# Eight additions of BP, eight products with AG and two products with GP taken from GpSimd to VectorE in the routing of a one-core decoder layer

## The chip, the cores and the metric

One core of a Trainium2 chip runs the whole kernel. The metric is the device time of one execution in microseconds, from which a median over runs is taken: 1073.58 us over three runs (1069.57 to 1077.26). In what follows PE is the engine of the matrix products (TensorE), PEld its loading of weights, DVE the vector engine, ACT the scalar engine, POOL GpSimd, and SP the engine whose queue issues most of the DMAs.

## The reference

One decoder layer over 1024 tokens of width 1024. A mixer with three branches gives `mix`; then

```python
x  = layernorm(alpha * x + (1 + gate1) * mix, ln1_g, ln1_b)
h2 = x * (1 + scale2) + shift2
logits = h2 @ w_router + b_router          # 32 experts
weights, experts = softmax(top4(logits))
ffn = sum over the 4 experts of weight * expert(h2)   # clamped SwiGLU, inner width 256
x  = layernorm(alpha * x + (1 + gate2) * ffn, ln2_g, ln2_b)
```

## The kernel before

Work goes in tiles of 128 tokens (t = 0 to 7) on the 128 partitions, everything in 32-bit floats; products that need the precision are made of three products of split halves (`mm3`, L224 to L226). The schedule is written by hand: each engine runs its instructions in the order in which the program issues them, and waits in that order.

Up to about 425 us the mixer runs. Then comes the routing, a loop over i = 2 to 7 (its body is printed below). In round i PE multiplies tile i of the mixer's output with `w_out` in two halves (`mix_mm`, 24 products each), while the tile u of the round before (u = i - 1; tiles 0, 1 and 2 are taken in rounds 2 and 3) is normalised and routed:

- `ln_half` and `stats` (L1005 to L1016, DVE) add the residual and take mean and variance; `norm` (L1029, ACT) writes the normalised row over x.
- `h2_mul` (L1033) makes h2 = x times GP, where GP is (1 + scale2) times the gain of the first norm. `h2_out` (L1038) adds BP, the shift that belongs to it, and SP stores the rows to HBM (L1039), from where the experts gather them. `y_scale` (L1042) multiplies x in place with AG, alpha times that gain: the residual that the output starts from.
- `logits` (L1049, PE) multiplies the transposed row with the router's weights into PSUM bank 7. `route` (L1055 to L1072) takes the best four experts and the mask M. `places_mm` (L1096, L1097, PE) counts with M how many earlier tokens chose each expert. `row_of` (L1140 to L1150) turns this into `idx`, rows of a table in HBM; its scratch lies in bank 7 too, so the logits of the next tile can't start until `idx` of the tile before is made. `to_table` has POOL write the four pairs per token with indirect DMAs (L1156).
- `y_mm` and `y_add` (L1173, L1179) add the experts' biases to the scaled row; SP stores it (L1182).

From round 5 on the weights of the first expert are split beside it (`units`, L1225 on ACT, L1228 on DVE). After the loop stands code without a loop, called the tail below (L1574 to L1660 or so): it routes tile 7 and runs the first three blocks of the experts (block = up to 128 rows of one expert) between the steps. It has its own product with GP (L1601, DVE) and addition of BP (L1623, POOL), splits two quarters of the second expert's weights on POOL (`hls[2][1](G)`, `hls[3][1](G)`, L1228), gathers rows (L1284, POOL), scales tile 7 (L1042, POOL) and orders the experts by size on DVE (L1500 to L1527). AG lies in memory that the down weights of the second expert take over (`dn`, L220 on ACT, L221 on DVE). Then the blocks of all experts follow until about 1000 us, and the second norm.

Before the change POOL makes all additions of BP and all products with AG, and the products with GP of tiles 1 and 2; DVE makes the other products with GP.

Of the kernel before, what the change touches and what calls it, by code (L numbers as in the profile page):

```python
# [146 lines left out]
def body(ctx, tc, A, out, offs, dbg=None):  # L147
    nc = tc.nc
    V, G, SC, PE, SY = nc.vector, nc.gpsimd, nc.scalar, nc.tensor, nc.sync
# [51 lines left out]
    def slot(kind, shape, dt=F32):  # L201
        n = turn[kind] = turn.get(kind, -1) + 1
        tag = SLOTS[kind][n % len(SLOTS[kind])]
        full = [shape[0], 2048 if tag[0] == "r" else 1024] if kind in ("x", "o", "xT", "gu") else None
        pool = keep if kind == "tt" else bigp if tag == "big" else mb[0] if kind in ("sg", "up", "gs") or tag[:2] == "dn" else ph
        if full and len(shape) > 2:
            full = [shape[0], shape[1], full[1] // shape[1]]
        return pool.tile(shape, dt, tag=tag, name=kind, bufs=COUNT.get(tag, 1), padded_shape=full)
# [76 lines left out]
    for i in range(5, 24):  # L285
        g, t = i // 8, i % 8
# [310 lines left out]
    for i in range(5, 24):  # L597
        g, t = i // 8, i % 8
# [349 lines left out]
    BP = pw.tile([P, D], F32, name="BP")  # L948
    r3 = rtile(3)
    GP, g2 = r3[:, :D], [r3[:, D:D + 512], r3[:, D + 512:]]  # L950
    AG = pw.tile([P, D], F32, name="AG")
# [42 lines left out]
    tk = {}  # L994
# [35 lines left out]

    def h2_mul(t):
        h2 = pw.tile([P, D], F32, tag="h2", name="h2", bufs=2)
        (G if t in (1, 2) else V).tensor_mul(h2, tk[t]["x"], GP)  # L1033
        tk[t]["h2"] = h2

    def h2_out(t):
        h2 = tk[t]["h2"]
        G.tensor_add(h2, h2, BP)  # L1038
        SY.dma_start(h2_d[blk(t + 1), :], h2)  # L1039

    def y_scale(t):
        G.tensor_mul(tk[t]["x"], tk[t]["x"], AG)  # L1042

    def logits(t, ks):
        if 0 in ks:
# [107 lines left out]
    def to_table(idx, pair):  # L1153
        for k in range(TOPK):
            G.memset(gap, 0.0)
            s_ = G.indirect_dma_start(out=tab_d, out_offset=bass.IndirectOffsetOnAxis(ap=idx[:, k:k + 1], axis=0),  # L1156
                                      in_=pair[:, k, :], in_offset=None)
            for o_ in scat:
                tc.declare_no_dep(s_.ins, o_.ins, reason="other rows of the table")
            scat.append(s_)  # L1160
# [131 lines left out]
    for i in range(2, NT):  # L1292
# [8 lines left out]
        if i == 3:  # L1301
            h2_mul(1)
            h2_out(1)
            y_scale(1)
            route_w(1)
            places_mm(1)
# [17 lines left out]
        if i == NT - 1:  # L1324
            gather(0)
        h2_mul(u)
        h2_out(u)
        y_scale(u)
        logits(u, range(KC))
        mix_mm(b, i, 1, range(2, 6))  # L1330
# [242 lines left out]
    t, w = NT - 1, NT - 2  # L1573
# [25 lines left out]
    x = tk[t]["x"]  # L1599
    h2 = pw.tile([P, D], F32, tag="h2", name="h2", bufs=2)  # L1600
# [19 lines left out]
    hls[0][1](V)  # L1620
    mring.allow(12)
    to_table(tk[t]["idx"], tk[t]["pair"])
    G.tensor_add(h2, h2, BP)  # L1623
    SY.dma_start(h2_d[blk(t + 1), :], h2)
    route_w(t)
    gu_mm(1)
# [10 lines left out]
    act_T(1, up)  # L1637
    gather(3)
    y_scale(t)
    gu_mm(2, range(0, 4))  # L1640
    for v in (w, t):
# [90 lines left out]
    with tc.For_i(0, n_over) as i:  # L1732
# [11 lines left out]
        x = slot("x", [P, D])  # L1744
# [124 lines left out]
```

## Time and profile before

| | |
|---|---|
| median of 3 runs | 1073.58 us |
| the profiled execution: its own time | 1075.12 us |
| the profiled execution: span from the first to the last instruction | 1073.3 us |
| PE busy in the span | 963.5 us (90%) |
| DVE busy | 812.4 us (76%) |
| ACT busy | 491.5 us (46%) |
| POOL busy | 370.8 us (35%) |
| mean granted clock of TensorE, as a share of full speed | 0.953 |

The profile is of one execution. A row of the chain or the timeline begins with the start of the instruction, counted from the start of the span, and its duration. What stands in brackets is the idle time of the engine just before it and what ended that. Shares of busy time are means over stages with different limits, so the routing is read by itself.

### The profile page before, as it was taken

The page shows a single profiled execution, that of the slowest core. Times are in us where ns is not written, and L with a number is a line of the kernel's source. Part 1 is how long each engine was busy: PE and PEld are TensorE (multiplying, and loading weights), DVE is VectorE, ACT ScalarE, POOL GpSimd, SP SyncE. Part 2 cuts the span into 40 slices and gives each one's busy share as a digit, 9 for nine tenths or more (in the row PEclk, how much of TensorE's full clock was granted, in tenths as well). Part 3 has the DMA queues.
Part 4 walks back from the last instruction along what each step waited for, and adds up shares of the span by engine and source line. Part 5 has one row for each costly group of instructions (what it writes and reads, how often), then busy time and mean ns, then how long its engine had stood idle before and what let it go on. Part 6 is the DMA issues. An engine that isn't in the chain of part 4 may idle for free. (4 is left out here: it accounts for less than half of the span.)

```text
span 1073.3 us, 14241 instructions
## 1 busy us (share of the span) xinstructions
PE 963.5 (90%) x4538; PEld 744.7 (69%) x4538; DVE 812.4 (76%) x1492; ACT 491.5 (46%) x788; POOL 370.8 (35%) x256
## 2 busy tenths in 40 slices
PE   5899999999999998699977999999998899997840
PEld 4777879778888777677866777777766577665520
DVE  5827669736577698757768689999979899888837
ACT  2263141322255444324452355665664556654636
POOL 2450011022000143677575322322433447544224
PEclk9899999999999999889989999999998999998975
DMA  9912127353443135314476989999989899998736
GB/s 311 325 47 79 60 79 258 111 196 125 140 144 103 45 106 183 103 40 143 158 255 217 272 256 299 338 297 320 286 274 298 247 327 302 306 279 263 236 71 270
DMA packets 115651, 219.20 MB, mean 204 GB/s; under 512 B 21166, under 2 KB 42680, under 8 KB 115576
## 3 DMA queue, kind: packets, MB, share of 16 engines
q1 hardware_dynamic: 99416, 181.50, 49.9%
q0 software_dynamic: 16160, 36.78, 14.9%
q8 instruction: 36, 0.59, 0.2%
q14 instruction: 39, 0.32, 0.1%
HBM read 187.27 MB, written 36.78 MB: 209 GB/s over the span
## 5 line engine op out<-in xcount | busy, mean ns | idle before, releaser
L1490 POOL DMA_INDIRECT y_d<-o,tt x46 | 88.4, 1922 | 197.6 <-DMA y_d<-o,tt 50.6
L1228 DVE TENSOR_TENSOR gu<-raw,gu 128x1024 fp32r<-128x1024 f32 x125 | 151.4, 1241 | 4.2 <-ACT gu L1225 3.9
L1225 ACT CAST gu<-raw 128x1024 fp32r<-128x1024 f32 x128 | 129.4, 1047 | 6.1 <-DMA raw<-in_w_gu 6.1
L1284 POOL DMA_INDIRECT x<-h_d,tt x46 | 91.8, 1996 | 92.2 <-PE bank L1396 67.1
L224 PE MATMUL bank<-gu,xT 128*128 128x512 f32 (+10 forms) x280 | 119.7, 428 | 0.0
L225 PE MATMUL bank<-gu,xT 128*128 128x512 f32 (+10 forms) x280 | 110.4, 394 | 2.1 <-DVE gu L1228 2.1
L226 PE MATMUL bank<-gu,xT 128*128 128x512 f32 (+10 forms) x280 | 110.9, 396 | 0.0
L226 PE MATMUL bank<-dn,aT 128*128 128x512 f32 (+11 forms) x184 | 75.6, 411 | 20.7 <-DVE aT L221 20.7
L224 PE MATMUL bank<-u,w 128*128 128x512 f32 x216 | 86.8, 402 | 0.0
L225 PE MATMUL bank<-u,w 128*128 128x512 f32 x216 | 85.3, 395 | 0.3 <-DVE u L221 0.3
L1484 DVE SCALAR_TENSOR_TENSOR o<-bank,tt,u 128x512 f32<-128x512 f32 (+11 forms) x92 | 65.5, 741 | 26.0 <-DMA y_d<-o,tt 17.9
L226 PE MATMUL bank<-u,w 128*128 128x512 f32 x216 | 85.0, 393 | 0.0
L220 ACT CAST dn<-raw 128x1024 fp32r<-128x1024 f32 x64 | 64.9, 1045 | 42.3 <-PE bank L226 35.1
L220 ACT CAST xT<-bank 128x512 fp32r<-128x512 f32 (+11 forms) x92 | 46.5, 508 | 76.5 <-PE bank L1396 74.5
L224 PE MATMUL bank<-w,u 128*128 128x512 f32 (+1 forms) x192 | 77.1, 402 | 2.8 <-ACT u L381 2.8
L221 DVE TENSOR_TENSOR dn<-raw,dn 128x1024 fp32r<-128x1024 f32 x64 | 76.0, 1213 | 2.9 <-ACT dn L220 2.6
L224 PE MATMUL bank<-dn,aT 128*128 128x512 f32 (+11 forms) x184 | 74.9, 407 | 0.4 <-ACT aT L220 0.4
L225 PE MATMUL bank<-dn,aT 128*128 128x512 f32 (+11 forms) x184 | 74.4, 404 | 0.0
L337 DVE SCALAR_TENSOR_TENSOR acc<-raw,cact,acc 128x512 f32<-128x512 f32 x80 | 68.2, 852 | 7.5 <-DMA raw<-in_w_ada 5.6
L226 PE MATMUL bank<-w,u 128*128 128x512 f32 (+1 forms) x192 | 71.5, 373 | 1.7 <-POOL u L382 1.6
L225 PE MATMUL bank<-w,u 128*128 128x512 f32 (+1 forms) x192 | 71.4, 372 | 1.1 <-DVE w L221 1.1
L224 PEld LDWEIGHTS bank<-gu,xT 128*128 128x128 f32 (+10 forms) x280 | 50.5, 180 | 18.9 <-issue 7.8
(419 smaller groups left out, 2197.5 us busy)
## 6 DMA issues: line engine op xcount, KB each, us to landing
raw<-in_w_gu SPq DMA_DIRECT2D x128, 512.0 KB
raw<-in_w_down SPq DMA_DIRECT2D x64, 512.0 KB
raw<-in_w_ada SPq DMA_DIRECT2D x32, 512.0 KB
raw<-in_w_ada SPq DMA_DIRECT2D x32, 256.0 KB
raw<-in_w_in SPq DMA_DIRECT2D x12, 512.0 KB
raw<-in_w_out SPq DMA_DIRECT2D x8, 512.0 KB
raw<-in_x SPq DMA_DIRECT2D x8, 512.0 KB
h_d<-h SPq DMA_DIRECT2D x8, 512.0 KB
```

Source lines behind the costliest of these rows:

```text
L220: SC.copy(hi, src)
L221: eng.tensor_tensor(lo, src, hi.bitcast(F32), op=ALU.subtract)
L224: PE.matmul(o, lh, rh, start=first, stop=False)
L225: PE.matmul(o, lh, rl, start=False, stop=False)
L226: PE.matmul(o, ll, rh, start=False, stop=last)
L337: V.scalar_tensor_tensor(acc, w[:, k, :], cact[:, kk:kk + 1], acc, op0=ALU.mult, op1=ALU.add)
L1225: SC.copy(hi_, r)
L1228: eng.tensor_tensor(lo_, r, hi_.bitcast(F32), op=ALU.subtract)
L1284: G.indirect_dma_start(out=x[:n], out_offset=None, in_=src, in_offset=bass.IndirectOffsetOnAxis(ap=segs[blocks[b]][:n, 0:1], axis=0), boun ...
L1484: V.scalar_tensor_tensor(o[:n, half_of(hf)], p_[:n], segs[s, i].bitcast(F32)[:n, 1:2], G2[:n, half_of(hf)], op0=ALU.mult, op1=ALU.mult)
L1490: G.indirect_dma_start(out=y_d, out_offset=bass.IndirectOffsetOnAxis(ap=segs[blocks[b]][:n, 0:1], axis=0), in_=outs.pop(b)[:n], in_offset= ...
```

## The change

Four lines: the calls of GpSimd (`G`) become calls of VectorE (`V`). The computation is the same; where the instructions stand in the program's order is the same too.

```diff
     def h2_mul(t):
         h2 = pw.tile([P, D], F32, tag="h2", name="h2", bufs=2)
-        (G if t in (1, 2) else V).tensor_mul(h2, tk[t]["x"], GP)
+        V.tensor_mul(h2, tk[t]["x"], GP)
         tk[t]["h2"] = h2

     def h2_out(t):
         h2 = tk[t]["h2"]
-        G.tensor_add(h2, h2, BP)
+        V.tensor_add(h2, h2, BP)
         SY.dma_start(h2_d[blk(t + 1), :], h2)

     def y_scale(t):
-        G.tensor_mul(tk[t]["x"], tk[t]["x"], AG)
+        V.tensor_mul(tk[t]["x"], tk[t]["x"], AG)
...
-    G.tensor_add(h2, h2, BP)
+    V.tensor_add(h2, h2, BP)
     SY.dma_start(h2_d[blk(t + 1), :], h2)
     route_w(t)
     gu_mm(1)
```

On DVE, at the start of round 3, the three instructions of tile 1 come to stand between `ln_half` of tile 3 and `route_w` of tile 1 (`raw` is x, `r` holds GP, `h` is h2, `es` the sum of the softmax):

```order
 L1005 SCALAR_TENSOR_TENSOR raw<-raw,bank 128x512
 L1006 BN_STATS stt<-raw 128x6
+L1033 TENSOR_TENSOR h_3934<-raw,r_3507 128x1024
+L1038 TENSOR_TENSOR h_3934<-h_3934,BP 128x1024
+L1042 TENSOR_TENSOR raw<-raw,AG 128x1024
 L1077 RECIPROCAL es<-es 128x1
 L1086 TENSOR_TENSOR bank<-bank,pairs 128x128
```

Three instructions are new ahead of everything that leads to `idx` of tile 1; the three of tile 2 follow right behind that `idx`, ahead of the tile's own route.

On DVE, in round 5 (tile 4; rounds 2, 4, 6 and 7 read alike), two instructions are new between the product with GP and the splitting of the expert's weights (`gu`) and the route:

```order
 L1006 BN_STATS stt<-raw 128x6
 L1033 TENSOR_TENSOR h_4372<-raw,r_3507 128x1024
+L1038 TENSOR_TENSOR h_4372<-h_4372,BP 128x1024
+L1042 TENSOR_TENSOR raw<-raw,AG 128x1024
 L1228 TENSOR_TENSOR gu<-raw,gu 128x1024
 L1055 SCALAR_TENSOR_TENSOR bank<-csv,q,bank 128x32
```

The route, which PE's counting waits for, stands behind them.

On DVE, in the tail, the addition for tile 7 comes between the splitting of the second expert's first quarter and `route_w`:

```order
 L221 TENSOR_TENSOR dn<-raw,dn 128x1024 x2
 L1228 TENSOR_TENSOR gu<-raw,gu 128x1024
+L1623 TENSOR_TENSOR h_4890<-h_4890,BP 128x1024
 L1086 TENSOR_TENSOR bank<-bank,pairs 128x128
 L1088 TENSOR_REDUCE bank<-bank 128x32
```

On POOL, at the same place, the two splits (L1228) and the gathers (L1284) move up behind the last write to the table:

```order
 L1155 MEMSET gap 1x1
 L1156 DMA tab_d<-pairs,idx 32768x2
-L1623 TENSOR_TENSOR h_4890<-h_4890,BP 128x1024
 L1228 TENSOR_TENSOR gu<-raw,gu 128x1024 x2
-L1284 DMA x<-h_d,tt 128x1024
-L1042 TENSOR_TENSOR raw<-raw,AG 128x1024
-L1284 DMA x<-h_d,tt 128x1024
+L1284 DMA x<-h_d,tt 128x1024 x2
```

POOL loses its 18 arithmetic instructions of the routing; DVE gains 18.

## Rows read from the trace of the kernel before

**Rows 1.** Stretches (us): busy PE, PEld, DVE, ACT, POOL (instructions), clock, DMA share, GB/s.

```profile
425.00:545.00 120.00, 105.48 (x541) 88.93 (x539) 81.61 (x254) 47.01 (x79) 78.75 (x73) 0.92 0.38 129
590.00:1073.30 483.30, 420.26 (x1944) 300.23 (x1943) 405.68 (x599) 272.72 (x399) 184.93 (x91) 0.94 0.90 275
```

**Rows 2.** PE's waits, timeline: start, duration, engine, line, operation, count, [idle before, releaser].

```profile
453.09 3.59 PE L1049 MATMUL bank<-wrg,xt 128*128 128x32 f32 x16 [8.42 <-DVE idx L1150]
...
468.70 1.94 PE L1049 MATMUL bank<-wrg,xt 128*128 128x32 f32 x16 [1.95 <-DVE idx L1150]
...
508.74 0.30 PE L1096 MATMUL bank<-M,ce 128*128 128x32 f32 x2
...
523.39 0.30 PE L1096 MATMUL bank<-M,ce 128*128 128x32 f32 x2
...
538.28 0.41 PE L1096 MATMUL bank<-M,ce 128*128 128x32 f32 x2
...
542.39 1.94 PE L1396 MATMUL bank<-ce,x 128*128 128x128 f32 x8 [2.93 <-DMA x<-h_d,tt]
...
574.03 0.50 PE L225 MATMUL bank<-gu,xT 128*128 128x512 f32 x1 [2.13 <-DVE gu L1228]
...
583.65 1.09 PE L1396 MATMUL bank<-ce,x 128*128 128x128 f32 x4 [3.43 <-DVE up L1428]
```

**Rows 3.** The instructions that move, grouped by line and shape, 425 to 600 us.

```profile
L1042 POOL TENSOR_TENSOR raw<-raw,AG 128x1024 f32<-128x1024 f32 x8 | 19.5, 2436 | 0.0
L1038 POOL TENSOR_TENSOR h<-h,BP 128x1024 f32<-128x1024 f32 x7 | 17.7, 2534 | 2.6 <-DVE h L1033 1.7 <-issue 0.6
...
L1033 DVE TENSOR_TENSOR h<-raw,r 128x1024 f32<-128x1024 f32 x5 | 6.1, 1227 | 2.2 <-ACT raw L1029 1.5 <-POOL r L976 0.7
```

**Rows 4.** DVE's timeline in the routing and the tail.

```profile
439.43 1.23 DVE L1033 TENSOR_TENSOR h<-raw,r 128x1024 f32<-128x1024 f32 x1 [0.74 <-POOL r L976]
440.57 0.25 DVE L1055 SCALAR_TENSOR_TENSOR bank<-csv,q,bank 128x32 f32<-128x32 f32 x1
...
442.41 4.02 DVE L980 SCALAR_TENSOR_TENSOR bdh<-tb,bdh 96x512 f32<-96x512 f32 x2
446.46 0.68 DVE L985 TENSOR_TENSOR bd<-bdh,bd 32x512 fp32r<-32x512 f32 x1
...
493.66 0.69 DVE L1005 SCALAR_TENSOR_TENSOR raw<-raw,bank 128x512 f32<-128x512 f32 x1 [2.99 <-PE bank L226]
...
506.61 0.29 DVE L1069 TENSOR_REDUCE M<-bank 128x32 f32<-128x128 f32 x1
...
521.54 0.29 DVE L1069 TENSOR_REDUCE M<-bank 128x32 f32<-128x128 f32 x1
...
537.93 0.29 DVE L1069 TENSOR_REDUCE M<-bank 128x32 f32<-128x128 f32 x1
...
569.38 4.60 DVE L1228 TENSOR_TENSOR gu<-raw,gu 128x1024 fp32r<-128x1024 f32 x1
...
575.80 1.29 DVE L1179 TENSOR_TENSOR raw<-raw,bank 128x512 f32<-128x512 f32 x2 [0.18 <-PE bank L1173]
```

**Rows 5.** POOL's timeline: two writes to the table, two splits in the tail.

```profile
530.00 0.97 POOL L1156 DMA_INDIRECT tab_d<-pairs,idx  x1 [0.22 <-issue]
...
532.56 1.85 POOL L1156 DMA_INDIRECT tab_d<-pairs,idx  x1 [0.21 <-issue]
...
568.16 4.72 POOL L1228 TENSOR_TENSOR gu<-raw,gu 128x1024 fp32r<-128x1024 f32 x2
```

**Rows 6.** SP's queue: the store of tile 6's h2.

```profile
541.37 0.33 SPq L1039 DMA_DIRECT2D h_d<-h  x1
```

**Rows 7.** ACT's timeline: the down weights of the second expert.

```profile
577.37 1.99 ACT L220 CAST dn<-raw 128x1024 fp32r<-128x1024 f32 x2 [7.22 <-POOL raw L1042]
```

**Rows 8.** Stretches behind two of PE's waits; columns as in rows 1.

```profile
453.09:460.10 7.01, 7.01 (x25) 6.24 (x26) 1.75 (x9) 0.39 (x2) 5.57 (x8) 0.50 0.03 3
...
468.70:474.00 5.30, 5.30 (x25) 4.53 (x26) 2.78 (x10) 1.94 (x4) 5.22 (x3) 0.68 0.04 18
```

## The prediction

> **What bounds the kernel now.** I read the stretches by stage first. In the routing, 425 to 545 us, PE is busy for 105.5 of 120 us, DVE for 81.6 and POOL for 78.8 [rows 1]: PE carries it, and a microsecond on DVE or POOL costs only where PE then stands. From 590 us on the DMA engines are 90% busy and PE 87% (420.26 of 483.30); weights are loaded as fast as slots come free. What is late at 590 us I take to be late at the end: the slots come free later by as much.
>
> Second, PE's own waits in time order [rows 2]. Between 444 and 590 us these matter: 8.42 and 1.95 us ahead of the logits (L1049) of tiles 1 and 2, both for `idx` of the tile before, which shares bank 7; 2.93 us for the first gathered rows; 2.13 us for a split weight (L1228); 3.43 us for the bank of a block's `up`. The last two lie in the tail. Everything else PE does without a gap.
>
> Third, DVE's timeline around these places [rows 4]. It shows two things: where DVE waits for PE (room for added work), and where an instruction takes far longer than its size asks (POOL is in its way).
>
> **The change part by part.** On POOL an addition takes 2.53 us and a product with AG 2.44 us; the product with GP, same shape, takes DVE 1.23 us [rows 3]. A follower that doesn't need its result starts 1.14 us after it began (439.43 to 440.57) [rows 4]. So mul, add, product in a row cost DVE 1.23 + 1.14 + 1.14 = 3.5 us, of which two new ones are 2.4 (1.23 + 1.14) where DVE made the first already. All 18 moved instructions come to about 18 x 1.2 = 21.6 us of DVE. Where does PE feel them?
>
> Round 2 (tile 0). The two new ones stand ahead of the route, +2.4 us. Behind it DVE's two L980 took 4.02 us; two instructions of that width (L985, half the columns of a whole row) take 0.68 each [rows 4], 1.4 together. The 2.6 us above that is POOL's addition and product, which run at the same time and now go. Net -0.2 us on the chain to `idx` of tile 0, where PE stands 8.42 us. Bounds: -0.3, and +2.4 if L980 stays slow for another reason.
>
> Round 3 (tiles 1 and 2). All three of tile 1 are new and stand between `ln_half` and everything that leads to `idx` of tile 1. PE waits for that `idx` already (1.95 us), so nothing hides them: +3.5 us. Queued behind them on DVE is `es`, for which ACT's softmax weights and then its copies and norm of tile 2 wait; these end ahead of the new `idx`. The three of tile 2 follow that `idx` while PE makes the logits and 18 products of `mix_mm`, which cover them. Bounds +3.4 to +3.7.
>
> The clock. Behind the 8.42 us wait the granted clock was 0.50 for 7.0 us (1.2 of 2.4 GHz), a loss of 3.5 us of full-speed work; behind the 1.95 us wait it was 0.68 over 5.3 us, a loss of 1.7 [rows 8]. The second wait becomes 5.5 us, between the two. The difference is 1.8 us; I take +0.5, since the nearer end by behaviour is the short wait (a single drop), and keep -0.4 to +1.8.
>
> Round 4: two new ones, +2.4 us on DVE, but it then waits 2.99 us for PE [rows 4]: 0. If that cover were gone it would cost 2.4.
>
> Rounds 5 and 6. PE's counting (L1096) needs M. M was ready at 506.61 + 0.29 = 506.90, with the new ones at 509.3; PE comes to it at 508.74 [rows 2, 4]: +0.6. In round 6: 521.54 + 0.29 + 2.4 = 524.2 against 523.39: +0.9 with the hop of 0.06 that round 7 shows (M at 538.22, PE at 538.28). Together +1.5 us; bounds 0.8 to 4.8 (nothing hidden).
>
> Round 7. M was just in time there, so +2.4 us; but PE stands 2.93 us for the first gathered rows right after [rows 2], which hides it, if these rows are not later themselves. They hang on POOL's four writes to the table for tile 5, the last of which took 1.85 us beside DVE's products, while a free one took 0.97 [rows 5]; they come 1.4 us later with `idx` of tile 5, about as late as PE. And SP's store of h2 at 541.37 [rows 6], which waited for POOL, goes some 3 us earlier, and the weight loads queued behind it too: they will run beside the gather. I take +0.3 us, bounds -0.5 to +3.
>
> The tail. The addition on DVE delays the transposed activations by 1.1 us (+0.7 on PE, which has 0.3 us of slack there by my reading). In return POOL's two splits (4.72 us from 568.16) start 2.4 us earlier, and DVE's split L1228, which took 4.60 us from 569.38 beside them, ends at about 572.0 instead of 573.98 [rows 4, 5]: PE's 2.13 us wait goes. Then the product with AG (1.14) stands ahead of L1179 at 575.80, and the chain from there to the 3.43 us wait runs on DVE without a gap. Net at that wait: 1.0 us earlier. ACT's wait of 7.22 us for AG's memory ends some 2 us earlier [rows 7], but DVE isn't waiting for ACT there: 0. Tail -1.0; bounds -5.6 (both PE waits go) to +3.7 (the addition comes to stand behind both of POOL's splits).
>
> Sum: -0.2 + 3.5 + 0.5 + 0 + 1.5 + 0.3 - 1.0 = +4.6 us. The profiled execution took 1075.12 us, so 1079.7; it lies 1.54 us above the median of the runs, so against that 1078.2, 0.4% more.
>
> The row shows an indirect DMA at 1.85 us beside DVE products and 0.97 alone [rows 5]. The Trainium skill, page "SBUF — State Buffer", section "Who interferes with whom", says that an instruction of DVE with two SBUF inputs contends only with a GpSimd instruction that reads SBUF, and that tensor_tensor did not stall DMAs that GpSimd issues. The row here disagrees, 0.9 us longer. By that rule the term for the gather would lose nothing or gain up to 0.9 us; by the row it stays.
>
> **The rivals.**
>
> *The tail gives back what the head costs* (not slower). POOL's arithmetic goes from the tail, and with it both waits of PE there: 2.13 + 3.43 = 5.6 us. For it: the 4.60 us of L1228 and ACT's 7.22 us behind POOL. Against: the second wait ends with a DVE chain in which two of the new instructions stand. It decides if the tail yields 5.6 or more: 5.6 - 5.6 = 0, own time 1075.1, 1073.6 against the median.
>
> *DVE becomes the bound.* Each new instruction is paid by PE: 18 x 1.2 = 21.6 us, 1095.2. For it: most stand ahead of `idx` or M, for which PE waits. Against: DVE waits 2.99 us for PE in round 4 [rows 4], and PE stands 2.93 us for the gathered rows in round 7 whatever DVE does [rows 2].
>
> *POOL's writes to the table are shut out.* In round 7 four products follow each other on DVE, 4.65 us (1.23 + 3 x 1.14). If the fourth write for tile 5 waits for all of them, it ends 3.6 us later than I have it, and so do the first rows: 4.6 + 3.6 = 8.2 us, 1081.8. For it: 1.85 against 0.97. Against: that one had two products beside it (0.9 us is less than one of them). The same page, section "SBUF: two separate sides", speaks of an exclusive lock held for a whole instruction, with the loser fully blocked: that is per instruction, and would go this way only if DVE wins each time.
>
> **How the numbers follow.** The forecast 0.50, the tail giving all back 0.20, DVE the bound 0.12, the shut-out 0.10; 0.08 for what I don't see. The forecast's own range is 1074 to 1083. The range takes in both near rivals, the unknown clock and 3 us of scatter between runs, and leaves DVE as the bound out: 1070 to 1088. A change of 1% (10.7 us) is about what a measurement of this kernel tells from none. Slower by more: 0.12 and a part of the forecast's upper end, 0.17. Faster by more: would need more than all waits of the tail, 0.04. Within: 0.79.
>
> **What would show it.** In the changed profile: PE's wait ahead of the logits of tile 2 at about 5.5 us instead of 1.95; that of tile 1 unchanged near 8.2; short waits of PE for M (L1069) in rounds 5 and 6, of 0.6 and 0.9; L980 at 1.4 us; L1228 of the tail at 1.2 us with no PE wait behind it; a wait near 3 us for `up` still there. I am wrong if the wait for tile 2 stays near 2 us, if PE waits over 2 us for M in each round, if the clock falls in rounds where it did not before, or if the stretch behind 590 us changes its length by more than 2 us.

## The result and the profile after

The changed kernel took 1083.45 us (median of 10 runs, 1078.82 to 1085.56), the kernel before in the same rounds 1074.13 (10 runs, 1069.57 to 1083.51). The ratio is 1.0072 [1.0052, 1.0092], or +7.7 us [+5.6, +9.9]. Forecast were 1078.2 us, +4.6, and a range of 1070 to 1088: right in sign and class (within 1%), too small in size. The forecast's own range, 1074 to 1083, just misses the measured median.

The profiled execution took 1083.21 us with a span of 1081.4, 8.1 more than the span before. First the stretches of the changed kernel; they answer to [rows 1]:

```profile
425.00:545.00 120.00, 102.46 (x515) 85.74 (x513) 90.48 (x252) 42.91 (x71) 37.62 (x57) 0.91 0.34 114
590.00:1081.40 491.40, 427.91 (x1965) 306.04 (x1965) 410.86 (x608) 274.19 (x400) 176.85 (x91) 0.93 0.90 275
```

POOL gave up half of its busy time (78.75 to 37.62 us), DVE took 8.87 more, and PE did less in the same 120 us: 515 matmuls instead of 541. The stretch behind 590 starts at a fixed time, and the changed kernel comes to it 6.3 us late (its wait for `up`, below, stands at 589.98 instead of 583.65), so 21 more matmuls lie in it. Counted from that wait it is 1.7 us longer.

PE's timeline, with the waits that answer to [rows 2]:

```profile
444.37 0.41 PE L1096 MATMUL bank<-M,ce 128*128 128x32 f32 x2 [1.59 <-DVE M L1069]
...
452.29 3.59 PE L1049 MATMUL bank<-wrg,xt 128*128 128x32 f32 x16 [7.28 <-DVE idx L1150]
...
470.84 3.59 PE L1049 MATMUL bank<-wrg,xt 128*128 128x32 f32 x16 [5.48 <-DVE idx L1150]
...
513.62 0.41 PE L1096 MATMUL bank<-M,ce 128*128 128x32 f32 x2 [0.47 <-DVE M L1069]
...
529.29 0.41 PE L1096 MATMUL bank<-M,ce 128*128 128x32 f32 x2 [0.73 <-DVE M L1069]
...
546.64 0.41 PE L1096 MATMUL bank<-M,ce 128*128 128x32 f32 x2 [2.41 <-DVE M L1069]
...
550.45 1.94 PE L1396 MATMUL bank<-ce,x 128*128 128x128 f32 x8 [2.07 <-DMA x<-h_d,tt]
...
558.13 1.97 PE L1049 MATMUL bank<-wrg,xt 128*128 128x32 f32 x16 [2.45 <-DVE idx L1150]
...
589.98 1.09 PE L1396 MATMUL bank<-ce,x 128*128 128x128 f32 x4 [3.43 <-DVE up L1428]
```

The wait for `idx` of tile 1 grew from 1.95 to 5.48 us, the waits for M are new, and the wait for L1228 in the tail is gone (a wait of 0.46 us for `aT` is left there). The wait for the first gathered rows is shorter (2.07 for 2.93), but it stands behind a new wait for M of 2.41: both together are longer than the one before.

From these landmarks comes the account, as distances on PE's timeline between the same instructions. "Again" are second profiled executions of both kernels (below).

| stretch on PE | before | after | more | again: before, after |
|---|---|---|---|---|
| start to logits of tile 1 | 453.09 | 452.29 | -0.80 | 450.83, 450.52 |
| to logits of tile 2 | 15.61 | 18.55 | +2.94 | 15.55, 19.58 |
| to counting (L1096) of tile 2 | 7.57 | 9.71 | +2.14 | 7.59, 10.26 |
| to counting of tile 3 | 17.19 | 17.17 | -0.02 | 17.18, 17.17 |
| to counting of tile 4 | 15.28 | 15.90 | +0.62 | 15.29, 15.90 |
| to counting of tile 5 | 14.65 | 15.67 | +1.02 | 14.65, 15.65 |
| to the first gathered rows | 19.00 | 21.16 | +2.16 | 19.04, 20.64 |
| to logits of tile 7 | 7.71 | 7.68 | -0.03 | 7.68, 7.69 |
| to the wait for `up` | 33.55 | 31.85 | -1.70 | 33.55, 33.49 |
| to the end | 489.7 | 491.4 | +1.7 | 488.9, 490.5 |

DVE's timeline, the moved instructions of tile 1 and those that answer to [rows 4]:

```profile
444.24 1.28 DVE L980 SCALAR_TENSOR_TENSOR bdh<-tb,bdh 96x512 f32<-96x512 f32 x2
...
463.98 1.21 DVE L1033 TENSOR_TENSOR h<-raw,r 128x1024 f32<-128x1024 f32 x1
465.22 1.22 DVE L1038 TENSOR_TENSOR h<-h,BP 128x1024 f32<-128x1024 f32 x1
466.37 1.22 DVE L1042 TENSOR_TENSOR raw<-raw,AG 128x1024 f32<-128x1024 f32 x1
467.50 0.16 DVE L1077 RECIPROCAL es<-es 128x1 f32<-128x1 f32 x1
...
497.92 0.69 DVE L1005 SCALAR_TENSOR_TENSOR raw<-raw,bank 128x512 f32<-128x512 f32 x1 [1.29 <-PE bank L226]
...
566.43 0.16 DVE L1150 SCALAR_TENSOR_TENSOR idx<-bank,pf 128x4 int32<-128x4 f32 x1
...
578.27 1.54 DVE L1228 TENSOR_TENSOR gu<-raw,gu 128x1024 fp32r<-128x1024 f32 x1
...
581.38 1.21 DVE L1042 TENSOR_TENSOR raw<-raw,AG 128x1024 f32<-128x1024 f32 x1
582.51 1.27 DVE L1179 TENSOR_TENSOR raw<-raw,bank 128x512 f32<-128x512 f32 x2
```

The three take 3.52 us from the start of the first to the start of `es` (463.98 to 467.50), and PE's wait grew by 3.53. L980 fell from 4.02 to 1.28 us, L1228 from 4.60 to 1.54, and DVE still waits 1.29 us for PE in round 4, so what was added there stayed covered.

### The profile page after: what moved, and what is told of

Its sections match the earlier page's. It is cut to its first block, busy times and chain, and to the rows that moved or that the text cites. A ratio compares the mean times of both kernels' runs of the same rounds, so it can differ in the third digit from the quotient of the medians.

```text
span 1081.4 us, 14234 instructions
## 1 busy us (share of the span) xinstructions
PE 965.0 (89%) x4538; PEld 744.4 (69%) x4538; DVE 824.1 (76%) x1510; ACT 492.5 (46%) x788; POOL 317.6 (29%) x238
## 5 line engine op out<-in xcount | busy, mean ns | idle before, releaser
L1228 DVE TENSOR_TENSOR gu<-raw,gu 128x1024 fp32r<-128x1024 f32 x125 | 148.6, 1219 | 4.3 <-ACT gu L1225 3.7
L1490 POOL DMA_INDIRECT y_d<-o,tt x46 | 84.9, 1846 | 213.5 <-DVE o L1484 36.5
L1284 POOL DMA_INDIRECT x<-h_d,tt x46 | 87.8, 1908 | 89.3 <-PE bank L1396 62.2
L221 DVE TENSOR_TENSOR dn<-raw,dn 128x1024 fp32r<-128x1024 f32 x64 | 76.1, 1215 | 3.3 <-ACT dn L220 2.6
L224 PE MATMUL bank<-w,u 128*128 128x512 f32 (+1 forms) x192 | 75.8, 395 | 3.0 <-ACT u L381 3.0
L226 PE MATMUL bank<-w,u 128*128 128x512 f32 (+1 forms) x192 | 70.8, 369 | 2.8 <-POOL u L382 2.7
L225 PE MATMUL bank<-w,u 128*128 128x512 f32 (+1 forms) x192 | 70.0, 365 | 1.1 <-DVE w L221 1.1
```

Source lines behind the costliest of these rows:

```text
L221: eng.tensor_tensor(lo, src, hi.bitcast(F32), op=ALU.subtract)
L224: PE.matmul(o, lh, rh, start=first, stop=False)
L225: PE.matmul(o, lh, rl, start=False, stop=False)
L226: PE.matmul(o, ll, rh, start=False, stop=last)
L1228: eng.tensor_tensor(lo_, r, hi_.bitcast(F32), op=ALU.subtract)
L1284: G.indirect_dma_start(out=x[:n], out_offset=None, in_=src, in_offset=bass.IndirectOffsetOnAxis(ap=segs[blocks[b]][:n, 0:1], axis=0), boun ...
```

## Experiments

The kernels of one group ran beside the kernel before on one chip. Ratios are to that. Microseconds are the ratio's part of about 1076. Only its second measurement below puts the changed kernel into a group; elsewhere a run is set against its +7.7, measured apart.

**Undo tiles 1 and 2.**

```diff
-        V.tensor_mul(h2, tk[t]["x"], GP)
+        (G if t in (1, 2) else V).tensor_mul(h2, tk[t]["x"], GP)
...
-        V.tensor_add(h2, h2, BP)
+        (G if t in (1, 2) else V).tensor_add(h2, h2, BP)
...
-        V.tensor_mul(tk[t]["x"], tk[t]["x"], AG)
+        (G if t in (1, 2) else V).tensor_mul(tk[t]["x"], tk[t]["x"], AG)
```

> The changed kernel with the three instructions of tiles 1 and 2 (product with GP, addition of BP, product with AG) given back to POOL; tiles 0 and 3 to 7 stay on DVE. Theory A (place in the order: the three of tile 1 stand ahead of idx of tile 1, PE waits for it, and the longer wait lowers the clock for longer): PE's wait ahead of the logits of tile 2 goes from 5.5 back to about 2 us, the clock at half speed behind it lasts about 3.4 us instead of 7, and some 5 us of the 7.7 us go: about 2.7 us above the kernel before. Rival B (DVE's load costs wherever it stands): 6 of 18 instructions go, a third of 7.7 us, so about 5.1 us above the kernel before.

Measured: 0.9985 [0.9967, 1.0004], -1.6 us, below both expectations and 9 us under the changed kernel. PE's timeline of this kernel, tile 2:

```profile
466.62 1.94 PE L1049 MATMUL bank<-wrg,xt 128*128 128x32 f32 x16 [1.94 <-DVE idx L1150]
...
474.22 0.30 PE L1096 MATMUL bank<-M,ce 128*128 128x32 f32 x2
```

The wait is back at 1.94, the logits behind it at 1.94 us instead of 3.59, and the way to the counting at 7.60 instead of 9.71. So the three of tile 1 cost more than their own time: the 2.1 us behind the wait go with it. The waits for M in the later rounds stayed (0.46, 0.77 and 2.40). By this profile the way on PE from the logits of tile 0 to the wait for `up` is still some 2 us longer than in the kernel before (table below), so the -1.6 us of the time are not explained by the trace.

**All on DVE, but tile 1's later.** The product and the addition of tile 1 stand behind `b_split(1)`, its product with AG behind the route of round 4.

```diff
-            h2_mul(1)
-            h2_out(1)
-            y_scale(1)
...
+        if i == 4:
+            y_scale(1)
...
+            h2_mul(1)
+            h2_out(1)
```

> The changed kernel with all 18 instructions on DVE, but tile 1's product with GP and addition of BP moved behind the second split of the bias matrix (b_split(1)) in round 3, and its product with AG behind the route of round 4. Theory A (place in the order): as with tiles 1 and 2 on POOL, PE's wait ahead of the logits of tile 2 about 2 us, about 5 us faster than the changed kernel, 2.7 us above the kernel before. Rival B (DVE's load): DVE does the same work, so nothing changes, 7.7 us above the kernel before.

Measured: 1.0036 [1.0017, 1.0055], +3.9 us. The wait is 1.95 and the way to the counting again 7.60. The product with AG isn't free at its new place: PE's wait for the scaled row (L1179) behind it grew from 1.19 to 2.10 us. The same 18 instructions are on DVE as in the changed kernel; where the three stand is worth some 4 us. That speaks for the place and against DVE's busy time. By the times the run before it, with six instructions fewer on DVE, is 5.5 us faster still; by the traces it is 1.1. A smaller price of DVE's load is not excluded.

**Who delays the first gathered rows.** In the changed kernel the first gather is issued at 542.68 and used at 550.45: 7.77 us. Before it was 537.89 and 542.39: 4.50. POOL's timeline of the changed kernel, the last write for tile 5 and the first two gathers, then SP's queue:

```profile
538.08 0.97 POOL L1156 DMA_INDIRECT tab_d<-pairs,idx  x1 [0.21 <-issue]
542.68 1.30 POOL L1284 DMA_INDIRECT x<-h_d,tt  x1 [3.63 <-issue]
544.29 1.22 POOL L1284 DMA_INDIRECT x<-h_d,tt  x1 [0.31 <-issue]
```

```profile
541.85 0.43 SPq L1039 DMA_DIRECT2D h_d<-h  x1
543.09 0.33 SPq L835 DMA_DIRECT2D raw<-in_w_down  x1
545.23 1.54 SPq L832 DMA_DIRECT2D raw<-in_w_gu  x3
```

The write isn't slowed (0.97), and the first gather is issued well ahead of PE. But the store of h2, 3.48 us behind the first gather's issue before [rows 6], now goes 0.83 us ahead of it, the loads follow, and POOL, free of its product, issues the second gather 1.6 us behind the first (5.9 us before). Three runs hold these back.

Loads alone (SP's loads wait behind `y_store`):

```diff
-            mring.allow(6)
...
-    mring.allow(9)
-    G2 = unit(13, F32)
-    SY.dma_start(G2, bcast(ada_d, D, 3072))
...
+    mring.allow(9)
+    G2 = unit(13, F32)
+    SY.dma_start(G2, bcast(ada_d, D, 3072))
```

> The changed kernel with five weight and vector loads of the end of the routing (second half of the first expert's down weights, three quarters of the second expert's weights, G2) queued on SP behind the store of tile 5's scaled row, so that they start after the first gathered rows have landed. Theory C (SP's loads, let go earlier, crowd the first gather): PE's wait for the gathered rows goes from 2.07 us to about 0 and the rows land some 2 to 3 us after their issue sooner than now (7.8 us from issue to PE's use now, 4.5 before); about 2 us faster than the changed kernel, 5.7 us above the kernel before. Rival D (POOL's second and third gather, which now follow the first at once, crowd it): no change, 7.7 us above.

The second and third gathers alone (behind POOL's split):

```diff
+    units[0][3]()
     gather(1)
     gather(2)
-    units[0][3]()
```

> The changed kernel with the second and third gather (blocks 1 and 2) moved on POOL behind its split of the first expert's last quarter, which waits for ACT, so that the first gather runs without them. Theory C (SP's loads crowd the first gather): no change, 7.7 us above the kernel before, 7.8 us from the first gather's issue to PE's use. Rival D (the two gathers crowd it): that distance falls to about 5 us, PE's wait for the rows to about 0, and the kernel is about 2 us faster than the changed one, 5.7 us above the kernel before.

Both, and the store of tile 6's h2 as well:

```diff
-        SY.dma_start(h2_d[blk(t + 1), :], h2)
+        if t < NT - 2:
+            SY.dma_start(h2_d[blk(t + 1), :], h2)
...
+    SY.dma_start(h2_d[blk(w + 1), :], tk[w]["h2"])
     mring.allow(9)
...
+    units[0][3]()
     gather(1)
     gather(2)
-    units[0][3]()
```

> The changed kernel with everything held that now starts beside the first gather: the loads as in the run that held the loads, the store of tile 6's h2 too (behind the store of tile 5's scaled row), and the second and third gather behind POOL's split. Theory C, widened (the store of h2, let go earlier by DVE, crowds the gather as the loads do): from the first gather's issue to PE's use about 4.5 us as in the kernel before (7.8 in the changed kernel, 6.8 with the loads held, 7.0 with the gathers held), PE's wait for the rows near 0, 2.1 us faster than the changed kernel, 5.6 us above the kernel before. Rival I (the gather is late for a reason of its own, not for other transfers): still about 6.8 us, no faster than with the loads held.

Measured: 1.0044 [1.0022, 1.0066], 1.0076 [1.0053, 1.0100] and 1.0034 [1.0013, 1.0055]. From issue to use the first gather took 6.75, 6.96 and 5.22 us, and only in the third run did PE not wait for it: neither theory C nor theory D holds by itself. Stretches of 3 us around the first rows (columns as in rows 1): the changed kernel, then loads held, gathers held, all held.

```profile
544.00:547.00 3.00, 0.59 (x5) 0.36 (x4) 2.45 (x11) 2.19 (x5) 2.22 (x2) 1.00 1.00 376
547.00:550.00 3.00, 1.38 (x5) 0.65 (x4) 2.50 (x8) 1.57 (x3) 0.00 (x0) 0.51 0.93 324
```

```profile
545.00:548.00 3.00, 0.58 (x6) 0.54 (x5) 2.33 (x12) 2.17 (x6) 2.22 (x2) 1.00 1.00 371
```

```profile
546.00:549.00 3.00, 0.82 (x5) 0.82 (x6) 2.30 (x13) 2.17 (x6) 0.00 (x0) 0.96 0.97 369
```

```profile
541.00:544.00 3.00, 1.03 (x5) 0.50 (x3) 2.14 (x10) 2.09 (x3) 0.78 (x1) 1.00 0.76 240
544.00:547.00 3.00, 2.57 (x12) 2.28 (x13) 2.37 (x11) 2.47 (x7) 0.00 (x0) 0.67 0.13 53
```

With loads or gathers alone held, the DMA engines are still full (371 and 369 GB/s): the other fills them. With all of it held they fall to 53 GB/s once the rows have come, and PE's way from the counting of tile 5 to the first rows is 18.73 us, under the 19.00 of the kernel before. This shows that the late rows are a collision of transfers, against rival I. The store of h2 wasn't held by itself, so its own part stays open. PE's timeline and POOL's of that last run:

```profile
544.43 0.41 PE L1097 MATMUL bank<-M,ce 128*128 128x32 f32 x2 [2.41 <-DVE M L1070]
545.79 1.91 PE L1396 MATMUL bank<-ce,x 128*128 128x128 f32 x8
```

```profile
540.57 1.21 POOL L1285 DMA_INDIRECT x<-h_d,tt  x1 [3.77 <-PE bank L226]
```

In the trace the gain isn't kept: what was held comes late, and the way from the logits of tile 7 to the wait for `up` is 35.17 us there, 31.85 in the changed kernel. By the times, with everything held the kernel is 4 us under the changed one, with the loads held 3 us, more than their traces show. Whether holding is of use as a cure stays open.

**Tiles 3 to 6 back on POOL** (addition and product with AG).

```diff
-        V.tensor_add(h2, h2, BP)
+        (G if 3 <= t <= 6 else V).tensor_add(h2, h2, BP)
...
-        V.tensor_mul(tk[t]["x"], tk[t]["x"], AG)
+        (G if 3 <= t <= 6 else V).tensor_mul(tk[t]["x"], tk[t]["x"], AG)
```

> The changed kernel with the additions of BP and products with AG of tiles 3 to 6 given back to POOL; tiles 0, 1, 2 and 7 stay on DVE. Theory G (in rounds 5 to 7 these hold up M, for which PE waits 0.47, 0.73 and 2.41 us, and the first gather is late): all three waits go, the first gather again takes about 4.5 us from issue to PE's use, and 0.6 + 1.0 + 2.1 = 3.7 us go: 4.0 us above the kernel before. Rival H (these waits are hidden by others, the cost is that of tile 1 and the clock alone): no change, 7.7 us above the kernel before.

Measured: 1.0009 [0.9986, 1.0032], +1.0 us, so rival H is out, and more is gone than theory G's 3.7 us. In tiles 4 to 6 no wait for M is left, and the first gather takes 4.61 us again (542.84 to 547.45), the way from the counting of tile 5 to it 19.18. So by the trace these eight instructions on DVE cost the 0.6 and 1.0 us of the waits for M and the 2.2 of the late rows; the further 3 us of the time I can't place. Tile 2's wait is 5.47 as in the changed kernel, and the way from the logits of tile 1 to the counting of tile 2 is 29.01 (28.26 and 29.84 in the changed kernel, 23.18 before).

**Tile 7 back on POOL.**

```diff
-        V.tensor_mul(tk[t]["x"], tk[t]["x"], AG)
+        (G if t == NT - 1 else V).tensor_mul(tk[t]["x"], tk[t]["x"], AG)
...
-    V.tensor_add(h2, h2, BP)
+    G.tensor_add(h2, h2, BP)
```

> The changed kernel with tile 7's addition of BP and product with AG (in the tail) given back to POOL; tiles 0 to 6 stay on DVE. Theory E (DVE and POOL shut each other out of SBUF in the tail): the distance on PE from the logits of tile 7 to the wait for up, 33.55 us before and 31.85 after the change, goes back to about 33.5; DVE's split L1228 beside POOL's two takes over 4 us again and PE waits about 2 us for it; 1.7 us slower than the changed kernel, 9.4 us above the kernel before. Rival F (two instructions less on DVE are simply a gain): 1 to 2 us faster than the changed kernel, 5.7 to 6.7 us above the kernel before.

Measured: 1.0068 [1.0043, 1.0094], +7.3 us: the times don't tell this from the changed kernel. The trace does, though its execution was the slowest of the seven (1094.0 us). PE's wait and DVE's split are as they were before:

```profile
585.91 0.50 PE L225 MATMUL bank<-gu,xT 128*128 128x512 f32 x1 [2.10 <-DVE gu L1228]
```

```profile
581.27 4.59 DVE L1228 TENSOR_TENSOR gu<-raw,gu 128x1024 fp32r<-128x1024 f32 x1
```

From the last `idx` of tile 7 to the wait for `up` it is 25.27 us here and 25.25 in the kernel before, 23.55 in the changed kernel and 23.56 with tiles 3 to 6 on POOL. The tail gives 1.7 us.

**Both kernels once more.** This asks how far two profiles of one program differ.

> The kernel before, unchanged, a second profiled execution of it. What is asked is how far two profiles of one program differ, stretch by stretch. Theory J (the routing is the same in every execution, the weight-bound stretch behind it is not): from the logits of tile 1 (453.09 in the first profile) to the wait for up (583.65) again 130.6 us within 0.5, from there to the end 489.7 with 1 to 2 us of scatter. Rival K (the weight-bound stretch repeats as well): 489.7 within 0.5, so that the 491.4 of the changed kernel is a cost of the change of 1.7 us. Ratio 1.000 by both.

> The changed kernel, unchanged, a second profiled execution. J: from the logits of tile 1 to the wait for up again 137.7 us within 0.5 (452.29 to 589.98 in the first), the tile 2 logits behind a 5.5 us wait and 9.7 us from them to the counting of tile 2, the gather again over 7 us from issue to use; behind the wait for up 489 to 492.5. K: 491.4 within 0.5 again. The ratio to before once more near 1.007 (+7.7 us); if it is under 1.004 the size to explain is smaller than I take it to be.

Measured: the kernel before against itself 1.0023 [1.0002, 1.0045], the changed one 1.0101 [1.0041, 1.0162] (4 runs). The first number is the lesson: 2.5 us between equal programs, with an interval that leaves 1 out. Differences of 2 to 3 us in the runs above aren't settled by their times alone, and I rest them on the traces. How far the two go together, with the mixed version and tile 0 alone from below: the way on PE from the logits of tile 0 to the wait for `up` in one profile each, its difference to the mean of the two profiles before (146.8), and the time.

| kernel | us on PE | more | more by time |
|---|---|---|---|
| before, two profiles | 146.3, 147.2 | | |
| changed, two profiles | 154.2, 156.3 | +7.4, +9.5 | +7.7, +10.9 |
| tiles 1 and 2 on POOL | 148.7 | +1.9 | -1.6 |
| tile 1 later | 149.8 | +3.0 | +3.9 |
| loads held | 153.6 | +6.9 | +4.7 |
| gathers held | 156.6 | +9.9 | +8.2 |
| all held | 154.0 | +7.2 | +3.7 |
| tiles 3 to 6 on POOL | 151.5 | +4.7 | +1.0 |
| tile 7 on POOL | 158.1 | +11.4 | +7.3 |
| mixed, two profiles | 143.7, 143.7 | -3.1, -3.1 | -10.4, -6.6 |
| tile 0 alone | 146.5 | -0.3 | -2.8 |

The order is much the same, but single rows differ by up to 7 us, and in most the time is better than the trace. Why, I don't know. The traces show where a cost lies; its size the times confirm no closer than that.

From the logits of tile 1 to the wait for `up` the kernel before took 130.53 us (130.56 in the first); theory J holds there. The changed one took 140.38 (137.69), and J fails: 3.2 us more lie where the clock was low (1.0 and 0.6 around tile 2, 1.6 at tile 7), 0.5 us less at the first rows. Stretches behind the wait for `idx` of tile 1 and at the logits of tile 7, in the changed kernel's first and second execution:

```profile
470.84:478.00 7.16, 7.16 (x25) 6.39 (x26) 5.79 (x13) 2.15 (x4) 4.46 (x8) 0.50 0.19 74
558.13:565.00 6.87, 6.87 (x33) 5.93 (x34) 2.96 (x11) 2.81 (x5) 5.12 (x8) 0.75 0.48 165
```

```profile
470.10:478.00 7.90, 7.90 (x27) 6.93 (x28) 5.79 (x13) 2.18 (x4) 4.44 (x8) 0.50 0.18 67
557.41:565.00 7.59, 7.58 (x27) 6.70 (x28) 2.89 (x10) 2.76 (x5) 4.29 (x8) 0.55 0.46 147
```

Behind the 5.5 us wait the granted clock is 0.50 over the whole stretch, 1.2 of 2.4 GHz, where it was 0.68 behind the short wait [rows 8]. All profiles bear this out: over the first 5.3 us behind the wait of about 5.5 us it was 0.50 in all seven that have it, and 0.62 to 0.74 in the seven that have the wait of about 2 us. At tile 7 the clock differs between two executions of the changed kernel (0.75 and 0.55), and the tail's 1.7 us didn't show on the way from the logits of tile 7 in the second. The stretch behind the wait for `up` was 488.6 to 493.7 us long in all profiles but one (496.7, tile 7 on POOL), and it moved by 0.7 and 0.9 us between two executions of one kernel, so K falls. I take its +1.7 in the table (+1.6 in the second pair) for scatter; that isn't shown, for the kernel before has two of the three shortest.

**A mixed version.** The kernel before, with tile 0's three on DVE behind `idx` of tile 0, the bias sums and the first split behind `route(1)`, and tile 7's two on DVE; POOL keeps tiles 1 to 6.

```diff
-        G.tensor_add(h2, h2, BP)
+        (V if t == 0 else G).tensor_add(h2, h2, BP)
...
-        G.tensor_mul(tk[t]["x"], tk[t]["x"], AG)
+        (V if t in (0, NT - 1) else G).tensor_mul(tk[t]["x"], tk[t]["x"], AG)
...
-        h2_mul(u)
-        h2_out(u)
-        y_scale(u)
+        if i > 2:
+            h2_mul(u)
+            h2_out(u)
+            y_scale(u)
...
-            b_sum(0)
-            b_sum(1)
-            b_split(0)
...
+            h2_mul(0)
+            h2_out(0)
+            y_scale(0)
             route(1)
+            b_sum(0)
+            b_sum(1)
+            b_split(0)
...
-    G.tensor_add(h2, h2, BP)
+    V.tensor_add(h2, h2, BP)
```

> A version that should beat both: the kernel before, with tile 0's three instructions on DVE but behind its idx (where DVE waits for PE), the sums of the bias matrix behind the route of tile 1, and tile 7's addition and product on DVE; tiles 1 to 6 on POOL as before. Theory A (what counts is what stands ahead of idx on DVE) and theory E (no POOL arithmetic beside DVE's split in the tail): PE's wait ahead of the logits of tile 1 falls from 8.4 to about 5.5 us, the distance in the tail from 33.55 to 31.85 us; together about 4.6 us below the kernel before (ratio 0.996). Rival B (DVE's load): five instructions more on DVE than before, so about 2 us above the kernel before.

> The mixed version without its part in tile 7: tile 0's product, addition and product with AG on DVE behind idx of tile 0, the sums and the split of the first block's weight behind route(1); tiles 1 to 7 as before. In the mixed version's profile the logits of tile 1 began 4.4 us earlier than before. Theory L (the two parts of the mixed version add up, and tile 7's part is worth the 1.7 us measured in the tail): -8.5 us, ratio 0.992, with L1228 back at 4.6 us and PE's wait of 2.1 us ahead of it. Rival M (the head is worth only what its wait lost, the rest of the mixed version's -10.4 us came from the tail): -4.4 us, ratio 0.996.

> The mixed version once more, in more rounds, since the kernel before measured against itself gave 1.0023 and tile 0's part alone 0.9974 (-2.8 us). Theory N (the -10.4 us was partly chance; the two parts add, head about -3 to -4, tail -1.7): about -5 us, ratio 0.995, and over 0.993. Rival O (tile 7's part is worth far more behind an early head than in the changed kernel, 7 us and more): ratio 0.990 to 0.992 again. In the profile by both: the logits of tile 1 12.9 us behind those of tile 0 (16.7 in the kernel before), L1228 at 1.5 us with no wait behind it, and from the last idx of tile 7 to the wait for up 23.5 us (25.2 before).

Measured: 0.9903 [0.9878, 0.9928], tile 0's part alone 0.9974 [0.9949, 1.0000], the mixed version again 0.9939 [0.9916, 0.9961]. It beats both kernels: the kernel before by 10.4 and 6.6 us side by side, the changed one, by its +7.7, by some 14 to 18. Its wait for tile 0's `idx` and its tail, PE's timeline of the last run:

```profile
434.44 1.86 PE L1049 MATMUL bank<-wrg,xt 128*128 128x32 f32 x16
...
447.38 3.60 PE L1049 MATMUL bank<-wrg,xt 128*128 128x32 f32 x16 [5.59 <-DVE idx L1150]
...
563.68 0.50 PE L226 MATMUL bank<-dn,aT 128*128 128x512 f32 x1 [0.43 <-DVE aT L221]
```

The logits of tile 1 begin 12.94 us behind those of tile 0 (15.76 and 16.68 in the kernel before), and PE no longer waits for L1228. For tile 0 alone (-2.8, at most -5.5 by its interval) L's -8.5 is out and M's -4.4 within it. The second measurement of the mixed version fits N; O's upper end, 0.992, lies in its interval, and the first measurement fits O, so O is less likely and not out. In the profile of tile 0 alone what the head won is lost again where the clock is low: 9.20 us from the logits to the counting of tile 2 (7.57 before; clock 0.59 over 8.4 us) and 35.15 from the logits of tile 7 to `up` (33.55 before; clock 0.53 over 7.3 us). The mixed version loses its tail's gain likewise: from the last `idx` to `up` it takes 23.56 and 23.57 us, but from the logits of tile 7, at a clock of 0.59 and 0.54, 33.45 and 33.48. That the two parts add isn't shown closer than the 2.5 us by which equal programs differ. By its profiles the mixed version is only some 2 us shorter (spans of 1071.0 and 1068.3 against 1073.3 and 1070.3): the two profiled executions of the kernel before (1075.1 and 1072.1 us) lie under most of its medians (1074.1 to 1078.3). What its other executions lose, and where, I haven't seen.

## Why the prediction came out as it did

*Round 2 (tile 0), -0.2.* Right. L980 ran at 1.28 us (1.4 expected). PE now waits 1.59 us for M of tile 0, and 7.28 instead of 8.42 for its `idx`; the distance of tile 1's logits from tile 0's is 16.49 us (15.76 and 16.68 before, 15.90 in the second execution after): no loss, though two executions of one kernel differ by more than the 0.2 us forecast.

*Round 3, tile 1's three, +3.5.* Right to 0.03 us: 5.48 against 1.95, nothing hid them, and two runs that take them from this place bring 1.94 and 1.95 back.

*The clock, +0.5.* This step failed: "the nearer end by behaviour is the short wait (a single drop)". A wait of 5.5 us behaved like the long one: 0.50 over at least 5.3 us in every profile that has it, as over 7.0 us after 8.42. From the logits of tile 1 to the counting of tile 2 the changed kernel needed 5.1 and 6.7 us more, 3.5 of which are the chain: the clock cost 1.6 and 3.2, the first still within my bounds of -0.4 to +1.8. Behind the longer wait itself it was 2.14 and 2.67, beyond them; behind the older wait, where I had priced nothing, the stretch came out 0.6 shorter and 0.5 longer than the 3.53 us more of waiting explain. I had read the clock behind a wait from the one execution I had. And at tile 7, where I had priced nothing, it fell further than before in the second execution (0.55; 0.72 over 6 us in both profiles before).

*Round 4, 0.* Right: 17.17 against 17.19.

*Rounds 5 and 6, +0.6 and +0.9.* Right: +0.62 and +1.02, in both executions.

*Round 7 and the first gather, +0.3, bounds -0.5 to +3.* Mis-sized: +2.16 and +1.60. I had named the cause ("they will run beside the gather") and gave it no price. M's 2.41 us is as forecast, and it would have been hidden had the rows come 4.5 us after their issue: 542.68 + 4.5 = 547.2, when PE had just counted. They came 3.3 us later, and 2.2 of these reached PE.

*The tail, -1.0.* Right in its parts, 0.7 short: L1228 fell to 1.54, its wait went, the wait for `up` stayed at 3.43. DVE's split ends 1.1 us behind the second of POOL's two both before (572.88 and 573.98) and after (578.73 and 579.81), so what it gained is that POOL's two came earlier. Counted from tile 7's last `idx`, L1228 ended 2.2 us earlier (2.0 forecast; 566.43 to 579.81 against 558.40 to 573.98), L1179 began 1.3 earlier behind the product with AG, and PE came to its wait for `up` 1.7 earlier. The 0.4 us between the last two lie in the small instructions that order the experts by size: from the first, L1500, to the `dn` behind them (L221) DVE took 2.90 us before, beside POOL's product with AG at first, and 2.53 after. L1500 before and after:

```profile
577.01 0.38 DVE L1500 SCALAR_TENSOR_TENSOR key<-bonus,cnt 32x32 f32<-32x32 f32 x1
```

```profile
583.71 0.17 DVE L1500 SCALAR_TENSOR_TENSOR key<-bonus,cnt 32x32 f32<-32x32 f32 x1
```

That POOL's product made them slow is likely and not shown.

*ACT's wait for AG's memory.* 7.22 us before [rows 7], 3.73 after, and nobody waited for it: 0, as forecast. The row of ACT's timeline:

```profile
582.62 2.00 ACT L220 CAST dn<-raw 128x1024 fp32r<-128x1024 f32 x2 [3.73 <-DVE raw L1042]
```

With the measured sizes the sum is 3.5 + 1.6 + 1.6 + 2.2 - 1.7 = +7.2 us for the first profile from the logits of tile 1 to the wait for `up` (+7.13 in the table), and +7.7 timed.

Against the forecast's 4.6 these are 2.6 us more: 1.1 for the clock, 1.9 for the first gather and 0.3 for small terms, less the 0.7 us by which the tail was too cautious. In part the errors offset each other; the range took in what was left since it had been set wide, for both near rivals and the scatter.

The rivals. *The tail gives all back:* no, the second wait stayed, as argued. *DVE the bound:* no; 21.6 us were moved, PE felt 3.5, 0.6 and 1.0 directly, and the run with the same 18 on DVE in a better order costs half. *POOL's writes shut out:* no, the fourth write took 0.97 us. But that hangs on 0.2 us: before the change DVE's product with GP began 0.22 us ahead of the write (1.85 us), after it 0.22 us behind.

```profile
532.34 1.22 DVE L1033 TENSOR_TENSOR h<-raw,r 128x1024 f32<-128x1024 f32 x1 [0.66 <-ACT raw L1029]
```

```profile
538.30 1.23 DVE L1033 TENSOR_TENSOR h<-raw,r 128x1024 f32<-128x1024 f32 x1 [1.07 <-ACT raw L1029]
```

Where the product begins first in the changed kernel, the write is long there too, in tile 6:

```profile
562.26 1.78 POOL L1156 DMA_INDIRECT tab_d<-pairs,idx  x1 [0.22 <-issue]
```

```profile
561.99 1.22 DVE L1601 TENSOR_TENSOR h<-raw,r 128x1024 f32<-128x1024 f32 x1
```

So my reading "beside DVE's products" left out which began first. Nor does a write wait for all products in a row, as the rival had it: before the change one took 2.01 us (517.69) with a product begun 0.06 us ahead of it and a second right behind that. The rival's price (+3.6) was near the 3.3 us by which the rows came late, through another door: loads and gathers, which the forecast had seen, not locks.

## What to carry to other kernels

When arithmetic is taken off an engine that also issues transfers, look at which transfers it was holding back: here a store, the loads behind it and two gathers started together, and the one that the critical engine waited for shared the DMA engines with some that nobody needed yet. Move instructions to the engine with the room at the place where it has room: the same 18 instructions cost 8 us where they stand ahead of a wait and 4 where three of them don't, and a choice by tile and place won 7 to 10 us by the times, 3 of which the traces show. A longer wait of PE cost more than its length here (3.5 us of wait, 1.6 and 3.2 more behind it): price the work behind it at the lower clock as well.

## What the runs showed that I had not expected

Holding back one of two competing streams changed little (371 and 369 GB/s against 376, first gather 6.75 and 6.96 us against 7.77); holding both and the store of h2 brought 5.22 or less. Two executions of one program differed by 1.6 us from tile 7's logits on, with the granted clock at 0.75 and 0.55 there (16 matmuls in 1.97 and in 3.39 us). And an indirect write of POOL was long by the order of two starts: in all 14 profiles it took 1.74 to 2.04 us where a DVE product, sum or split of 128x1024 with both inputs in SBUF had begun at most 0.32 us ahead of it, and 0.96 to 0.98 us where one began only behind it, even 0.01 us behind.
